# Stage 2 loads keys and values piece by piece, the last stage's first tiles lie beside it in SBUF, and out-projection begins with the first 1024 tokens

## Chip, cores and metric

One core of a Trainium2 chip runs the whole block. The metric is the device time of one execution in microseconds (us); of several runs the median stands.

## What is computed

One layer over 2048 tokens of width 1024, in float32. The reference, cut:

```python
h = _rmsnorm(x, ln1_g[l])
p = h @ w_in[l]
y_rwkv = _rwkv7_time_mix(p[..., :RWKV_COLS], ...)      # 8 heads x 64, recurrent over tokens
y_sb = _stick_breaking_attention(p[..., RWKV_COLS:], sb_gain[l])
x = x + jnp.concatenate([y_rwkv, y_sb], axis=-1) @ w_out[l]
h = _rmsnorm(x, ln2_g[l])
x = x + jnp.square(jax.nn.relu(h @ w_up[l])) @ w_down[l]
...
# in _stick_breaking_attention, for each block of queries:
z = jnp.einsum('bhqd,bhkd->bhqk', q[:, :, start:end], k[:, :, :end]) * scale
log_beta = jax.nn.log_sigmoid(z)
log_keep = jnp.where(causal, log_beta - z, 0.0)
log_a = log_beta + lax.cumsum(log_keep, axis=3, reverse=True) - log_keep
att = jnp.where(causal, jnp.exp(log_a), 0.0)
outs.append(jnp.einsum('bhqk,bhkd->bhqd', att, v[:, :, :end]))
```

Attention is causal: the output of the first tokens needs only the first keys and values.

## The kernel before, in words

Three stages follow each other; DRAM tensors carry data between them.

**Stage 1** projects the input and runs the recurrence, in four blocks of 512 tokens with two halves each. Its last part is `chain` of block 3, half 1: four chunks (names 310 to 313), each a row of small dependent steps: matmuls `Xp` (L557), `R` on VectorE (L570), `Up` (L572), a copy to `UV` on ScalarE (L573), `Sp` (L577), the state `S` on VectorE (L579). No later chunk can begin before `S` of the one before. Results go to the DRAM tensors `yd`, `vrd`, `bond`.

**Stage 2** is the attention: 4 query blocks b of 512, 4 pairs of heads hp, and for each the key blocks j = b down to 0, which makes 40 steps (b,hp,j). A step has four **fronts** (128 queries each): matmuls `z` (L271, L273), two sigmoids `keep` and `ga` on ScalarE (L275, L277), a scan `E` on VectorE (L281), a product into `ga` on GpSimd (L282). One step later come its **backs**: transposes `tr` (L297), a copy `th` on VectorE or ScalarE (L301, L302), matmuls into `OT` (L304). At the end of a (b,hp) `finish` copies OT (`ots`, L308), transposes it (`o`, L310), copies it (`osb`, L312) and stores it in the DRAM tensor `sbd` (L313). All 16 key tiles and 16 value tiles of the whole sequence stay in SBUF, and `load` fetches each once.

**Stage 3** begins with the out-projection. For each of 16 token tiles of 128, `mixed` loads `y` (from `yd` and `sbd`), `v`, `g` and `b` and normalizes y: means and squares (L86 to L93), a power on GpSimd (L96), products (L97 to L103). `prep` transposes y (`ytr`, L115) and splits it into `yh` and `yl` (L116, L117). `outproj` makes 2 x 24 matmuls `op` per tile (L30 to L32) against the weights `wo` (high half) and `wol` (low half). The weights come as eight pieces `wor` of 512 KB through two slots, called `xin`; each piece is converted on ScalarE (L199, L205) and subtracted on VectorE or GpSimd (L200, L206). The tiles of one half (1024 tokens) come first and go to the DRAM tensor `x2d`; those of the other stay in SBUF (`acc`) and go on to the MLP (`up`, `down`), which then takes the first half from `x2d`. Before, the half that came first was tokens 1024 to 2047.

The order on each engine is made by a scheduler from the data dependences, the memory that tiles share, and its own timing model; engines and the SP queue then run in that order. Pools have a left and a right side of SBUF. A tile whose memory overlaps that of an earlier pool waits for the tiles there.

Of the kernel before, what the change touches and what calls it, by code (L numbers as in the profile page):

```python
# [8 lines left out]
F32 = mybir.dt.float32  # L9
# [47 lines left out]
        nc.scalar.copy(hi,ps)  # L57
        nc.vector.tensor_tensor(out=lo,in0=ps,in1=hi.bitcast(F32),op=ALU.subtract)

def stage3(tc,consts,x,ys,w_out,g2,w_up,w_down,gf,gnw,gnb,gaincol,out,x2d,VB=1):  # L60

    yd,vrd,bond,gd,sbd=ys
    nc=tc.nc; V=nc.vector; P=nc.gpsimd; A=nc.scalar; TE=nc.tensor
    with ExitStack() as ctx:
        rctx=ExitStack()
        rp=rctx.enter_context(tc.tile_pool(name="s3r",bufs=1,reuse_waits="tile",side="right"))
        wol=rp.tile([128,8,1024],F32R,name="wol")
        gnwb=rp.tile([128,512],F32,name="gnw"); gnbb=rp.tile([128,512],F32,name="gnb")
        nc.sync.dma_start(out=gnwb,in_=gnw.to_broadcast([128,512]))
# [33 lines left out]
            V.tensor_tensor(out=yr,in0=yr,in1=gt_,op=ALU.mult)  # L103
            return yt
        def prep(half,tt,sp,rp):
            gt=half*8+tt
            yt=mixed(gt,sp,rp)
            xt=rp.tile([128,1024],F32,tag="xin",name=f"x3_{gt}",bufs=2)
            nc.sync.dma_start(out=xt,in_=x[128*gt:128*gt+128])
            yh=sp.tile([128,8,128],F32R,tag="yh",name=f"yh{gt}",bufs=2)  # L110
            yl=sp.tile([128,8,128],F32R,tag="yl",name=f"yl{gt}",bufs=2)
            for g in range(2):
                ps=pp.tile([128,4,128],F32,tag="tr",name=f"ytr{gt}{g}",bufs=2)
                for j in range(4):
                    TE.transpose(ps[:,j],yt[:,128*(4*g+j):128*(4*g+j+1)],consts['ident'])  # L115
                A.copy(yh[:,4*g:4*g+4],ps)  # L116
                V.tensor_tensor(out=yl[:,4*g:4*g+4],in0=ps,in1=yh[:,4*g:4*g+4].bitcast(F32),op=ALU.subtract)  # L117
            return yh,yl,xt
        def outproj(half,tiles,wo):

            for n in range(2):
                for tt,(yh,yl,xt) in tiles:
                    gt=half*8+tt; dst=xt if half else accs[0][tt]
                    ps=pp.tile([128,512],F32,tag="dn",name=f"op{gt}{n}",bufs=3)
                    for kt in range(8):
                        mm3(nc,ps,yh[:,kt],yl[:,kt],wo[0][n][kt],wo[1][:,kt,512*n:512*n+512],kt==0,kt==7)
                    V.tensor_tensor(out=dst[:,512*n:512*n+512],in0=ps,in1=xt[:,512*n:512*n+512],op=ALU.add)
                    if half and n: nc.sync.dma_start(out=x2d[128*tt:128*tt+128],in_=dst)
# [33 lines left out]
        def final(half,tt,sp):  # L162

            a=accs[half][tt]
            o=sp.tile([128,1024],F32,tag="xn" if tt%2 or not half else "wdf",name=f"fo{half}{tt}",bufs=2)
            ssq=sp.tile([128,2],F32,tag="ssqf",name=f"fssq{half}{tt}",bufs=4)
            for n in range(2):
                sl=slice(512*n,512*n+512)
                A.activation(o[:,sl],a[:,sl],AF.Square,accum_out=ssq[:,n:n+1])  # L169
            rs=sp.tile([128,1],F32,tag="rsf",name=f"frs{half}{tt}",bufs=4)  # L170
            P.tensor_tensor(out=rs,in0=ssq[:,0:1],in1=ssq[:,1:2],op=ALU.add)  # L171
            P.tensor_scalar(rs,rs,1.0/D,1e-5,ALU.mult,ALU.add)  # L172
            P.tensor_tensor(out=rs,in0=rs,in1=consts['mhalf'],op=ALU.pow)  # L173
            r0=1024*half+128*tt
            for n in range(2):
                sl=slice(512*n,512*n+512)
                if n and tt<7:
                    A.activation(o[:,sl],a[:,sl],AF.Copy,scale=rs)
                    P.tensor_tensor(out=o[:,sl],in0=o[:,sl],in1=gfb[:,sl],op=ALU.mult)  # L179
                else: V.scalar_tensor_tensor(out=o[:,sl],in0=a[:,sl],scalar=rs,in1=gfb[:,sl],op0=ALU.mult,op1=ALU.mult)  # L180
                nc.sync.dma_start(out=out[r0:r0+128,sl],in_=o[:,sl])
# [62 lines left out]
def stage2(tc,consts,kd,qd,vd,sbd,cfg=None):  # L244

    nc=tc.nc; V_=nc.vector; A=nc.scalar; P=nc.gpsimd; TE=nc.tensor
    g=dict(GA=9,E=6,TH=4,QB=3,DV=(1,4,7))
    g.update(cfg or {})
    with ExitStack() as ctx:
        sp=ctx.enter_context(tc.tile_pool(name="s2",bufs=1,reuse_waits="tile"))  # L250
# [5 lines left out]
        for k in keeps: P.memset(k[:,:,512:513],1.0)  # L256

        pad=pp.tile([128,1],F32,name="pad"); V_.memset(pad,0.0)
        kv={}; cnt=[0,0]
        def load(hp,j):  # L260
            K=sp.tile([128,512],F32,name=f"K{hp}{j}"); V=sp.tile([128,4,128],F32,name=f"V{hp}{j}")
            nc.sync.dma_start(out=K,in_=kd[hp][:,512*j:512*j+512])
            nc.sync.dma_start(out=V,in_=vd[hp][:,4*j:4*j+4])
            kv[hp,j]=(K,V)
        def front(b,hp,j,Q,carry,i):

            n=f"{b}{hp}{j}"; K=kv[hp,j][0]
            W=128*(i+1) if j==b else 512; o=512-W
            z=pz.tile([128,2,512],F32,tag="z",name=f"z{n}{i}",bufs=2)
            for h in range(2):  # L270
                TE.matmul(z[:,h,0:W],lhsT=Q[64*h:64*h+64,128*i:128*i+128],rhs=K[64*h:64*h+64,0:W],start=True,stop=j<b,skip_group_check=True)  # L271
            if j==b:
                for h in range(2): TE.matmul(z[:,h,W-128:W],lhsT=consts['identr'],rhs=consts['cmask'],start=False,stop=True,skip_group_check=True)  # L273
            s=keeps[cnt[0]%2]; cnt[0]+=1
            A.activation(s[:,:,o:512],z[:,:,0:W],AF.Sigmoid,scale=-0.125)  # L275
            ga=sp.tile([128,2,512],F32,tag="ga",name=f"ga{n}{i}",bufs=g['GA'])
            A.activation(ga[:,:,o:512],z[:,:,0:W],AF.Sigmoid,scale=0.125)  # L277
            E=sp.tile([128,2,513],F32,tag="E",name=f"E{n}{i}",bufs=g['E'])
            for h in range(2):
                init=1.0 if j==b else carry[i][h]  # L280
                V_.tensor_tensor_scan(E[:,h,o:513][:,::-1],s[:,h,o:513][:,::-1],pad.to_broadcast([128,W+1]),init,ALU.mult,ALU.bypass)  # L281
            P.tensor_tensor(out=ga[:,:,o:512],in0=ga[:,:,o:512],in1=E[:,:,o+1:513],op=ALU.mult)  # L282
            carry[i]=[E[:,h,o:o+1] for h in range(2)]
            return ga,o
        def back(b,hp,j,gas,OT,kt):

            n=f"{b}{hp}{j}"; V=kv[hp,j][1]
            i0=kt if j==b else 0; q0=128*i0
            for u in range(2):

                c0=max(i0,2*u)
                if c0>=2*u+2: continue
                tr=pt.tile([128,2,256],F32,tag="tr",name=f"tr{n}{kt}{u}",bufs=2)
                for h in range(2):
                    for i in range(c0,2*u+2):
                        ga,o=gas[i]
                        TE.transpose(tr[:,h,128*(i-2*u):128*(i-2*u)+128],ga[:,h,o+128*kt:o+128*kt+128],consts['ident'])  # L297
                th=sp.tile([128,2,256],F32,tag="th",name=f"th{n}{kt}{u}",bufs=g['TH'])
                q=slice(128*(c0-2*u),256); qq=slice(128*c0,256*u+256)
                cnt[1]+=1  # L300
                if cnt[1]%8 in g['DV']: V_.tensor_copy(out=th[:,:,q],in_=tr[:,:,q])  # L301
                else: A.copy(th[:,:,q],tr[:,:,q])  # L302
                for h in range(2):
                    TE.matmul(OT[64*h:64*h+64,qq],lhsT=V[:,kt,64*h:64*h+64],rhs=th[:,h,q],start=j==b and kt==0 and u==0,stop=j==0 and kt==3 and u==1,skip_group_check=True)  # L304
        def finish(b,hp,OT):
# [4 lines left out]
            for i in range(4): TE.transpose(o[:,i],ots[:,128*i:128*i+128],consts['ident'])  # L310
            osb=sp.tile([128,4,128],F32,tag="osb",name="osb"+n,bufs=2)
            A.copy(osb,o)  # L312
            nc.sync.dma_start(out=sbd[512*b:512*b+512,128*hp:128*hp+128].rearrange("(i p) d -> p i d",i=4),in_=osb)  # L313

        late=[None]
        def step(new):
            prev,late[0]=late[0],new
            for i in range(4):
                if new:
                    b,hp,j,Q,carry,gas,st=new  # L320
                    gas.append(front(b,hp,j,Q,carry,i))
                if prev:
                    b,hp,j,Q,carry,gas,st=prev
                    if j==b and i==0: st.append(pp.tile([128,512],F32,tag="OT",name=f"OT{b}{hp}",bufs=1))
                    back(b,hp,j,gas,st[0],i)
                    if j==0 and i==3: finish(b,hp,st[0])
        for b in range(4):
            for hp in range(4):
                load(hp,b)
                Q=sp.tile([128,512],F32,tag="Q",name=f"Q{b}{hp}",bufs=g['QB'])  # L330
                nc.sync.dma_start(out=Q,in_=qd[hp][:,512*b:512*b+512])
                carry=[None]*4; st=[]
                for j in range(b,-1,-1): step((b,hp,j,Q,carry,[],st))
        step(None)

def sb_consts(tc,cp,c):
# [332 lines left out]
def hybrid_block(tc, x, smalls, w_in, wd, wa, wg, g1, g2, gnw, gnb, w_out, w_up, w_down, gf, out):  # L669
    nc = tc.nc  # L670
    with ExitStack() as ctx:
# [13 lines left out]
        with tc.tile_pool(name="c1", bufs=1, reuse_waits="tile") as c1:  # L685
            rw_consts(tc, c1, c, smalls, wd, wa)
            stage1(tc, c, x, w_in, kd, qd, vd, scr, yd, vrd, bond, gd, wg, g1)
        stage2(tc, c, kd, qd, vd, sbd)
        stage3(tc, c, x, (yd, vrd, bond, gd, sbd), w_out, g2, w_up, w_down, gf, gnw, gnb, c["gain"], out, x2d)


def columns(a):
# [37 lines left out]
```

## Time and profile before

| | |
|---|---|
| median of 3 runs | 3343.86 us (3341.51 to 3344.73) |
| the profiled execution's own time | 3338.49 us |
| its span, first to last instruction | 3336.7 us |
| TensorE (PE) busy | 3166.1 us, 95% of the span |
| VectorE (DVE), GpSimd (POOL), ScalarE (ACT) busy | 2010.7, 1245.4, 1167.7 us |
| mean granted TensorE clock | 0.969 of full |

Stage 1 ends with the chain at about 1115 us, stage 2 runs from there to about 1665, out-projection to about 1920, the MLP to the end. The profile's shares are means over all of these; the two joints between the stages are read in their own stretches.

### The profile page before, as it was taken

To read this page: it belongs to the slowest core of one execution; us is meant where nothing else is said; L and a number is where in the kernel's file an instruction comes from. 1 tells how busy PE (TensorE), PEld (TensorE's weight loads), DVE (VectorE), ACT (ScalarE), POOL (GpSimd) and SP (SyncE) were. 2 spreads that over 40 slices of the span, in tenths; PEclk is the share of its full clock that TensorE was granted. 3 is DMA by queue.
4 is the path that set the end of the run, shared out by engine and by line. 5 is a ranking of instruction groups with operands and counts; after the bars stand their busy time and mean duration, and the time that the engine had idled before them with its cause. 6 is when DMAs were issued, how large, how long until landed. Compare 5 with 4: busy or idle time off the path is not lost. (4 is left out here: it accounts for less than half of the span.)

```text
span 3336.7 us, 45433 instructions
## 1 busy us (share of the span) xinstructions
PE 3166.1 (95%) x17504; PEld 2398.0 (72%) x17504; DVE 2010.7 (60%) x3139; ACT 1167.7 (35%) x2192; POOL 1245.4 (37%) x1089
## 2 busy tenths in 40 slices
PE   8999999999998799999959999999999999999998
PEld 6677767777777544444448788888888888888887
DVE  4674575476375477778566555555555755555555
ACT  4434443443442476667522221111111411111112
POOL 5444444443442354555455432222222422222223
PEclk9999999999998799999979999999999999999999
DMA  3342242232232400000065221111111421111111
GB/s 100 101 120 74 85 131 75 83 121 83 73 100 66 136 23 17 14 10 7 4 199 165 89 76 51 51 45 45 45 51 48 158 79 51 51 45 45 44 44 63
DMA packets 146729, 239.30 MB, mean 72 GB/s; under 512 B 50000, under 2 KB 58192, under 8 KB 146512
## 3 DMA queue, kind: packets, MB, share of 16 engines
q1 hardware_dynamic: 146512, 236.39, 22.7%
q8 instruction: 138, 2.26, 0.3%
q14 instruction: 79, 0.65, 0.1%
HBM read 190.14 MB, written 46.20 MB: 71 GB/s over the span
## 5 line engine op out<-in xcount | busy, mean ns | idle before, releaser
L160 DVE TENSOR_TENSOR acc<-acc,dn 128x512 f32<-128x512 f32 x512 | 344.5, 685 | 411.2 <-PE dn L32 405.6
L282 POOL TENSOR_TENSOR ga<-ga,E 128x1024 f32<-128x1024 f32 (+3 forms) x160 | 274.5, 1726 | 275.6 <-ACT ga L277 124.5
L145 ACT ACTIVATE r<-up 128x512 f32<-128x512 f32 x128 | 75.6, 592 | 615.4 <-PE up L32 615.4
L148 DVE TENSOR_TENSOR m<-r 128x512 f32<-128x512 f32 x128 | 190.9, 1492 | 113.5 <-ACT r L145 113.5
L281 DVE TENSOR_TENSOR_SCAN E<-keep,E,pad 128x513 f32<-128x513 f32 x192 | 232.4, 1263 | 36.4 <-ACT keep L275 36.4
L304 PE MATMUL OT<-th,V 128*64 128x256 f32 (+1 forms) x1152 | 179.5, 392 | 18.2 <-DVE th L301 17.8
L297 PEld LDWEIGHTS tr<-ident,ga 128*128 128x128 f32 x1088 | 114.5, 140 | 105.6 <-issue 94.1
L297 PE MATMUL tr<-ident,ga 128*128 128x128 f32 x1088 | 181.5, 287 | 5.4 <-DVE th L301 2.2
L271 PE MATMUL z<-K,Q 64*128 64x512 f32 (+3 forms) x640 | 159.8, 582 | 11.4 <-DMA Q<-qd 7.7
L275 ACT ACTIVATE keep<-z 128x1024 f32<-128x1024 f32 (+3 forms) x160 | 144.7, 906 | 72.1 <-PE z L273 31.0
L149 DVE TENSOR_TENSOR gl<-m,gh 128x512 fp32r<-128x512 f32 x128 | 148.4, 1160 | 11.6 <-ACT gh L146 0.9
L277 ACT ACTIVATE ga<-z 128x1024 f32<-128x1024 f32 (+3 forms) x160 | 143.7, 904 | 29.1 <-PE tr L297 28.4
L304 PEld LDWEIGHTS OT<-th,V 128*64 128x64 f32 x1152 | 57.6, 134 | 103.4 <-issue 40.1
L302 ACT COPY th<-tr 128x512 f32<-128x512 f32 (+1 forms) x180 | 101.2, 566 | 75.8 <-PE tr L297 74.7
L386 POOL TENSOR_TENSOR wls<-wfs,whs 128x512 fp32r<-128x512 f32 x64 | 84.3, 1318 | 109.1 <-ACT whs L385 100.8
L281 DVE TENSOR_TENSOR_SCAN E<-keep,pad 128x129 f32<-128x129 f32 (+3 forms) x128 | 97.6, 806 | 42.0 <-ACT keep L275 31.1
L535 DVE TENSOR_TENSOR tm<-Am,Xs 128x240 f32<-128x240 f32 (+27 forms) x248 | 106.1, 428 | 23.4 <-DMA Am<-scrA 17.1
L536 DVE TENSOR_TENSOR Xs<-Xs,tm 128x240 f32<-128x240 f32 (+27 forms) x248 | 113.5, 458 | 6.3
L30 PE MATMUL ips<-hT,whs 128*128 128x512 f32 x256 | 108.4, 423 | 0.5 <-ACT whs L385 0.4
L32 PE MATMUL ips<-hT,wls 128*128 128x512 f32 x256 | 107.9, 421 | 0.6 <-POOL wls L386 0.6
L301 DVE COPY th<-tr 128x512 f32<-128x512 f32 (+1 forms) x108 | 69.8, 647 | 63.1 <-PE tr L297 57.9
L30 PE MATMUL op<-wo,yh 128*128 128x512 f32 x256 | 103.4, 404 | 3.3 <-ACT yh L116 3.3
(1265 smaller groups left out, 8675.6 us busy)
## 6 DMA issues: line engine op xcount, KB each, us to landing
wfs<-w_in SPq DMA_DIRECT2D x64, 256.0 KB, 2.9
x<-x SPq DMA_DIRECT2D x32, 256.0 KB, 3.0
wfr<-w_in SPq DMA_DIRECT2D x32, 256.0 KB, 2.7
wfk<-w_in SPq DMA_DIRECT2D x32, 256.0 KB, 2.7
wfv<-w_in SPq DMA_DIRECT2D x32, 256.0 KB, 2.7
wfsv<-w_in SPq DMA_DIRECT2D x32, 256.0 KB, 2.8
x<-x SPq DMA_DIRECT2D x16, 512.0 KB, 3.6
out<-fo SPq DMA_DIRECT2D x32, 256.0 KB, 2.4
```

The lines of the kernel that those rows point to most:

```text
L30: nc.tensor.matmul(ps,lhsT=lh,rhs=rh,start=first,stop=False)
L148: V.tensor_tensor(out=m,in0=r,in1=r,op=ALU.mult)
L149: V.tensor_tensor(out=gl[:,bl],in0=m,in1=gh[:,bl].bitcast(F32),op=ALU.subtract)
L160: V.tensor_tensor(out=a,in0=a,in1=ps,op=ALU.add)
L271: TE.matmul(z[:,h,0:W],lhsT=Q[64*h:64*h+64,128*i:128*i+128],rhs=K[64*h:64*h+64,0:W],start=True,stop=j<b,skip_group_check=True)
L275: A.activation(s[:,:,o:512],z[:,:,0:W],AF.Sigmoid,scale=-0.125)
L277: A.activation(ga[:,:,o:512],z[:,:,0:W],AF.Sigmoid,scale=0.125)
L281: V_.tensor_tensor_scan(E[:,h,o:513][:,::-1],s[:,h,o:513][:,::-1],pad.to_broadcast([128,W+1]),init,ALU.mult,ALU.bypass)
L282: P.tensor_tensor(out=ga[:,:,o:512],in0=ga[:,:,o:512],in1=E[:,:,o+1:513],op=ALU.mult)
L297: TE.transpose(tr[:,h,128*(i-2*u):128*(i-2*u)+128],ga[:,h,o+128*kt:o+128*kt+128],consts['ident'])
L304: TE.matmul(OT[64*h:64*h+64,qq],lhsT=V[:,kt,64*h:64*h+64],rhs=th[:,h,q],start=j==b and kt==0 and u==0,stop=j==0 and kt==3 and u==1,skip_gr ...
L536: V.tensor_tensor(out=X[:,0:m,i+1:],in0=X[:,0:m,i+1:],in1=tm[:,0:m,i+1:],op=ALU.add)
```

## The change

`stage2` keeps four slots of keys and four of values and loads a piece for each step, 40 of each in place of 16; the queries have two slots in place of three; the store of `osb` is issued by ScalarE and not by SP. The right-side pool of stage 3 (`s3r`: the low weights `wol`, the inputs of `mixed`, `xin`, and now `yh` and `yl`) is opened before stage 2. The half that out-projection takes first is now tokens 0 to 1023. The amount of arithmetic is the same.

```diff
-def stage3(tc,consts,x,ys,w_out,g2,w_up,w_down,gf,gnw,gnb,gaincol,out,x2d,VB=1):
+def stage3(tc,consts,x,ys,w_out,g2,w_up,w_down,gf,gnw,gnb,gaincol,out,x2d,rp,rctx,VB=1):
...
-        rctx=ExitStack()
-        rp=rctx.enter_context(tc.tile_pool(name="s3r",bufs=1,reuse_waits="tile",side="right"))
...
-            gt=half*8+tt
+            gt=8-half*8+tt
...
-            yh=sp.tile([128,8,128],F32R,tag="yh",name=f"yh{gt}",bufs=2)
-            yl=sp.tile([128,8,128],F32R,tag="yl",name=f"yl{gt}",bufs=2)
+            yh=rp.tile([128,8,128],F32R,tag="yh",name=f"yh{gt}",bufs=2)
+            yl=rp.tile([128,8,128],F32R,tag="yl",name=f"yl{gt}",bufs=2)
...
-            r0=1024*half+128*tt
+            r0=1024*(1-half)+128*tt
...
-    g=dict(GA=9,E=6,TH=4,QB=3,DV=(1,4,7))
+    g=dict(GA=9,E=6,TH=4,QB=2,DV=(1,4,7),KV=4)
...
-        def load(hp,j):
-            K=sp.tile([128,512],F32,name=f"K{hp}{j}"); V=sp.tile([128,4,128],F32,name=f"V{hp}{j}")
+        def load(b,hp,j):
+            n=f"{b}{hp}{j}"
+            K=sp.tile([128,512],F32,tag="K",name="K"+n,bufs=g['KV']); V=sp.tile([128,4,128],F32,tag="V",name="V"+n,bufs=g['KV'])
             nc.sync.dma_start(out=K,in_=kd[hp][:,512*j:512*j+512])
             nc.sync.dma_start(out=V,in_=vd[hp][:,4*j:4*j+4])
-            kv[hp,j]=(K,V)
+            return K,V
...
-            nc.sync.dma_start(out=sbd[512*b:512*b+512,128*hp:128*hp+128].rearrange("(i p) d -> p i d",i=4),in_=osb)
+            A.dma_start(out=sbd[512*b:512*b+512,128*hp:128*hp+128].rearrange("(i p) d -> p i d",i=4),in_=osb)
...
-                load(hp,b)
...
-                for j in range(b,-1,-1): step((b,hp,j,Q,carry,[],st))
+                for j in range(b,-1,-1): step((b,hp,j,Q,*load(b,hp,j),carry,[],st))
...
+        rctx = ExitStack()
+        rp = rctx.enter_context(tc.tile_pool(name="s3r", bufs=1, reuse_waits="tile", side="right"))
         stage2(tc, c, kd, qd, vd, sbd)
```

Lines of the changed kernel stand up to two numbers lower than those named above in the rows of order that follow.

On PE, in chunk 310 of the last chain (z0000 is z of b=0, hp=0, j=0, front 0), the order before was:

```order
L557 MATMUL Xp310_10571<-S_165,AR313_9519 128x128
L572 MATMUL Up310_10580<-R310_10579,XT31_9692 32x64 x8
L569 MATMUL Xp310_10571<-UV310_9270,P13100_9362 32x64 x2
L569 MATMUL Xp310_10571<-UV310_9270,P13110_9449 32x64 x2
L569 MATMUL Xp310_10571<-UV310_9270,P13120_9536 32x64 x2
L569 MATMUL Xp310_10571<-UV310_9270,P13130_9580 32x64 x2
```

And now:

```order
L555 MATMUL Xp310_10571<-S_165,AR313_9519 128x128
L270 MATMUL z0000_10862<-K000_10858,Q00_10856 128x128 x2
L272 MATMUL z0000_10862<-cmask_97,identr_95 128x128 x2
L270 MATMUL z0001_10874<-K000_10858,Q00_10856 128x256 x2
L272 MATMUL z0001_10874<-cmask_97,identr_95 128x128 x2
L570 MATMUL Up310_10580<-R310_10579,XT31_9692 32x64 x8
L270 MATMUL z0002_10886<-K000_10858,Q00_10856 128x384 x2
```

The z of 11 fronts (0000 to 0003, 0100 to 0103, 0200 to 0202) now stand among the matmuls of chunks 310 and 311; before, the first stood behind the last chunk. Their ScalarE, VectorE and GpSimd rows moved with them: in these two chunks 20 sigmoids stand between ScalarE's copies of the chain.

On VectorE, right behind the last state `S` of the chain, now (gm0 and gm1 are means of the out-projection's tiles 0 and 1, th00011 a copy of a back of stage 2):

```order
L577 TENSOR_TENSOR S_165<-SD313_10775,Sp313_10808 64x4x64 x2
L300 COPY th00000_10934<-tr00000_10929 128x512
L280 SCALAR_TENSOR_TENSOR E0203_11119<-keep1_10851,pad_10854 128x513 x2
L198 TENSOR_TENSOR wol_15484<-wor00_15515,wo00_15517 128x2x512
L84 TENSOR_REDUCE gm0_15565<-y3_0_15556 128x8
L300 COPY th00011_10971<-tr00011_10966 128x512
L85 TENSOR_SCALAR gm0_15565<-gm0_15565 128x8
L86 TENSOR_TENSOR y3_0_15556<-y3_0_15556,gm0_15565 128x512
L84 TENSOR_REDUCE gm1_15618<-y3_1_15609 128x8
L280 SCALAR_TENSOR_TENSOR E0300_11154<-keep0_10850,pad_10854 128x129 x2
```

Four rows further on stands `ots00`, the finish of the first (b,hp). Before, the rows of wol, gm and y stood behind the last `ots33` of stage 2. All of `mixed` for tiles 0 and 1, up to the last product (L103), now stands inside stage 2; SP has the loads for it, and pieces wor00 to wor02, between the loads of keys and values.

On SP, in the middle of stage 2, the loads now run V202, Q21, K212, V201, K211, V200 (the steps run 202, 201, 200, 212, 211): a key piece is issued beside the value piece of two steps before. There were no such loads here before.

On PE, at the end of stage 2, now (op00 is tile 0, column half 0):

```order
L309 MATMUL o33_15472<-ident_60,ots33_15470 128x128 x4
L113 MATMUL ytr00_15595<-ident_60,y3_0_15556 128x128 x4
L113 MATMUL ytr01_15602<-ident_60,y3_0_15556 128x128 x4
L30 MATMUL op00_15715<-wo00_15517,yh0_15593 128x512
L31 MATMUL op00_15715<-wol_15484,yh0_15593 128x512
L113 MATMUL ytr10_15648<-ident_60,y3_1_15609 128x128 x4
```

Before, the transposes of tile 8 stood here, whose y was loaded behind the last store of stage 2. Pieces wor03 and wor10 to wor13 are still loaded behind the last key and value loads, each when a slot is free.

## Rows read from the trace of the kernel before

**Rows 1.** The page's head and its part 1 (busy us, share, instructions).
```profile
span 3336.7 us, 45433 instructions
...
PE 3166.1 (95%) x17504; PEld 2398.0 (72%) x17504; DVE 2010.7 (60%) x3139; ACT 1167.7 (35%) x2192; POOL 1245.4 (37%) x1089
```

**Rows 2.** Windows: length, busy us of PE, PEld, DVE, ACT, POOL, clock, DMA.
```profile
1050.00:1115.00 65.00, 49.45 (x511) 42.83 (x509) 11.85 (x25) 11.48 (x20) 5.01 (x10) 0.65 0.12 33
...
1150.00:1175.00 25.00, 24.16 (x150) 12.45 (x150) 19.62 (x27) 18.22 (x28) 13.74 (x10) 1.00 0.11 33
1175.00:1200.00 25.00, 22.89 (x143) 11.12 (x141) 19.56 (x24) 17.13 (x27) 13.55 (x9) 1.00 0.11 33
...
1665.00:1708.00 43.00, 3.36 (x17) 2.40 (x14) 23.87 (x26) 13.16 (x21) 20.49 (x13) 0.57 0.65 207
```

**Rows 3.** Timeline, joint of stages 1 and 2: start, us, engine, line, idle before.
```profile
1064.18 1.16 PE L557 MATMUL Xp<-S,AR 128*128 128x128 f32 x8
...
1113.35 1.91 PE L582 MATMUL Xp<-UV,P 128*64 128x64 f32 x16
1122.92 0.80 PE L271 MATMUL z<-K,Q 64*128 64x128 f32 x4 [7.66 <-DMA Q<-qd]
...
1148.91 0.66 PE L310 MATMUL o<-ident,ots 128*128 128x128 f32 x4 [0.80 <-DVE ots L308]
```

**Rows 4.** Timeline, joint of stages 2 and 3, PE and the fourth `op` sum.
```profile
1663.93 1.40 PE L304 MATMUL OT<-th,V 128*64 128x256 f32 x8
...
1703.04 1.97 PE L115 MATMUL ytr<-ident,y 128*128 128x128 f32 x8 [36.26 <-DVE y L103]
1707.59 0.80 PE L30 MATMUL op<-wo,yh 128*128 128x512 f32 x1 [2.58 <-ACT yh L116]
...
1740.60 0.68 DVE L127 TENSOR_TENSOR x<-op,x 128x512 f32<-128x512 f32 x1
```

**Rows 5.** Timeline, the same joint, other engines.
```profile
1667.84 0.50 SPq L69 DMA_DIRECT2D gnw<-gnw  x1
...
1680.71 0.68 DVE L86 TENSOR_REDUCE gm<-y 128x8 f32<-128x512 f32 x1
...
1692.16 2.35 POOL L26 TENSOR_TENSOR wu00l<-wu00f,wu00h 128x1024 fp32r<-128x1024 f32 x1
1692.22 3.37 DVE L97 TENSOR_TENSOR y<-y,gs 128x1024 f32<-128x1024 f32 x1 [1.18 <-POOL gs L96]
```

**Rows 6.** Tile wor: ns min/median/max, first and last start us; landing times.
```profile
L200 DVE TENSOR_TENSOR wol<-wor,wo x2: 1224/1224/1225, 1679.6 to 1703.9; 128x1024 fp32r<-128x1024 f32 x2
L200 POOL TENSOR_TENSOR wol<-wor,wo x2: 2339/2352/2365, 1681.0 to 1707.1; 128x1024 fp32r<-128x1024 f32 x2
...
DMA to landing us min/median/max: 3.8/5.4/10.0
```

**Rows 7.** Tile op, the first of its three kinds of matmul.
```profile
L30 PE MATMUL op<-wo,yh x256: 389/395/796, 1707.6 to 1917.7; 128*128 128x512 f32 x128
```

**Rows 8.** Groups by line and form, 1120 to 1665 us: busy us, mean ns, idle before.
```profile
L275 ACT ACTIVATE keep<-z 128x1024 f32<-128x1024 f32 x112 | 115.7, 1035 | 39.2 <-PE z L271 21.7 <-PE z L273 7.9 <-issue 2.5
...
L275 ACT ACTIVATE keep<-z 128x256 f32<-128x256 f32 x16 | 6.4, 399 | 7.6 <-PE z L273 7.4
```

**Rows 9.** Lines 93, 97 and 103: ns min/median/max, first and last start us.
```profile
L93 DVE TENSOR_REDUCE gs<-gsq x64: 403/411/421, 1684.9 to 1889.1; 128x4 f32<-128x256 f32 x64
L97 DVE TENSOR_TENSOR y<-y,gs x16: 1217/1226/3369, 1692.2 to 1896.7; 128x1024 f32<-128x1024 f32 x16
L103 DVE TENSOR_TENSOR y<-y,g x16: 675/682/692, 1702.3 to 1900.2; 128x512 f32<-128x512 f32 x16
```

**Rows 10.** Part 5 of the page, the products of stage 2 on GpSimd.
```profile
L282 POOL TENSOR_TENSOR ga<-ga,E 128x1024 f32<-128x1024 f32 (+3 forms) x160 | 274.5, 1726 | 275.6 <-ACT ga L277 124.5
```

**Rows 11.** DMA issues from 1150 to 1660 us: KB each, us to landing; and line 313's issue.
```profile
Q<-qd SPq DMA_DIRECT2D x10, 256.0 KB, 2.6
...
L313 SPq DMA_DIRECT2D sbd<-osb x16: 359/360/370, 1150.2 to 1667.4; - x16
```

More of the change, by code (lines that the diff above doesn't have):

```diff
@@ L122, in outproj @@
                 for tt,(yh,yl,xt) in tiles:
-                    gt=half*8+tt; dst=xt if half else accs[0][tt]
+                    gt=8-half*8+tt; dst=xt if half else accs[0][tt]
                     ps=pp.tile([128,512],F32,tag="dn",name=f"op{gt}{n}",bufs=3)
@@ L258, in stage2, with front @@
         pad=pp.tile([128,1],F32,name="pad"); V_.memset(pad,0.0)
-        kv={}; cnt=[0,0]
-        def load(hp,j):
-            K=sp.tile([128,512],F32,name=f"K{hp}{j}"); V=sp.tile([128,4,128],F32,name=f"V{hp}{j}")
+        cnt=[0,0]
+        def load(b,hp,j):
+            n=f"{b}{hp}{j}"
+            K=sp.tile([128,512],F32,tag="K",name="K"+n,bufs=g['KV']); V=sp.tile([128,4,128],F32,tag="V",name="V"+n,bufs=g['KV'])
             nc.sync.dma_start(out=K,in_=kd[hp][:,512*j:512*j+512])
             nc.sync.dma_start(out=V,in_=vd[hp][:,4*j:4*j+4])
-            kv[hp,j]=(K,V)
-        def front(b,hp,j,Q,carry,i):
-            n=f"{b}{hp}{j}"; K=kv[hp,j][0]
+            return K,V
+        def front(b,hp,j,Q,K,carry,i):
+            n=f"{b}{hp}{j}"
             W=128*(i+1) if j==b else 512; o=512-W
@@ L284, in front, with back @@
             return ga,o
-        def back(b,hp,j,gas,OT,kt):
-            n=f"{b}{hp}{j}"; V=kv[hp,j][1]
+        def back(b,hp,j,V,gas,OT,kt):
+            n=f"{b}{hp}{j}"
             i0=kt if j==b else 0; q0=128*i0
@@ L319, in step @@
                 if new:
-                    b,hp,j,Q,carry,gas,st=new
-                    gas.append(front(b,hp,j,Q,carry,i))
+                    b,hp,j,Q,K,V,carry,gas,st=new
+                    gas.append(front(b,hp,j,Q,K,carry,i))
                 if prev:
-                    b,hp,j,Q,carry,gas,st=prev
+                    b,hp,j,Q,K,V,carry,gas,st=prev
                     if j==b and i==0: st.append(pp.tile([128,512],F32,tag="OT",name=f"OT{b}{hp}",bufs=1))
-                    back(b,hp,j,gas,st[0],i)
+                    back(b,hp,j,V,gas,st[0],i)
                     if j==0 and i==3: finish(b,hp,st[0])
@@ L687, in hybrid_block @@
             stage1(tc, c, x, w_in, kd, qd, vd, scr, yd, vrd, bond, gd, wg, g1)
+        rctx = ExitStack()
+        rp = rctx.enter_context(tc.tile_pool(name="s3r", bufs=1, reuse_waits="tile", side="right"))
         stage2(tc, c, kd, qd, vd, sbd)
-        stage3(tc, c, x, (yd, vrd, bond, gd, sbd), w_out, g2, w_up, w_down, gf, gnw, gnb, c["gain"], out, x2d)
+        stage3(tc, c, x, (yd, vrd, bond, gd, sbd), w_out, g2, w_up, w_down, gf, gnw, gnb, c["gain"], out, x2d, rp, rctx)
 def columns(a):
```

## Prediction

> **What bounds the kernel now.** I read the page first: PE is busy 95% of 3336.7 us [rows 1], so time can only come from stretches where PE stands still, and those have to be found by place. The windows show two. At the joint of stages 1 and 2 PE is busy 49 of 65 us at a mean clock of 0.65, while DVE and ACT are busy 12 and 11 us [rows 2]: every engine waits for another one's small step. The timeline shows this chain ending at 1115.26 us (1113.35 + 1.91) and the first z at 1122.92, after 7.66 us of waiting for the load of Q [rows 3]. At the joint of stages 2 and 3 PE is busy 3.4 of 43 us while the DMA moves 207 GB/s [rows 2]. The last OT ends at 1665.33, the next transposes begin at 1703.04 after an idle 36.26 us that VectorE's last product of `mixed` ended, and the first op stands at 1707.59 [rows 4]. Everything that this product needs (loads, squares, power) begins only behind stage 2's last store [rows 5]. Between the joints PE is busy 47.05 of 50 us at full clock (the two windows from 1150 [rows 2]), so there is little to win there and something to lose.
>
> **The joint of stages 2 and 3.** Take T as the end of the last OT. Before, the fourth op sum (tiles 0 and 1 of the order, both column halves) is taken out of PSUM from 1740.60, which is T + 75.3 [rows 4]. Now y of two tiles is ready at T, and half of the weights' pieces are loaded. What is late next is the rest of the weights. Five pieces are left, through two slots, and one slot takes wor03, wor11 and wor13 one after the other, each when the one before is converted. T to the end of wor01's conversion: `ots`, `o`, two `ytr`, two `yh`, the cast and GpSimd's subtraction of 2.35 us [rows 6], which I put at 7 us. Then three rounds of landing (median 5.4 us [rows 6]) and conversion (a cast of about 1 us, a subtraction of 1.22 or 2.35 [rows 6], and a place in the queue: 4.4 together): 3 x 9.8 = 29.4. Behind the last piece come 6 matmuls of tile 0 and 24 of tile 1; out-projection's 768 matmuls take 210.1 us (1707.6 to 1917.7 [rows 7], transposes included), 0.27 each, so 8 us. Sum: T + 44.4, against T + 75.3: a gain of 30.9. Out-projection started at a low clock before, and the stop-and-go start now will give some of that again: I take 28. Bounds: with landings of 3.8 us the sum is T + 40 (gain 36), with 10.0 T + 58 (gain 17) [rows 6]. Later tiles cost what they did; PE sets their pace, and the swap of halves only changes which rows are loaded.
>
> **The joint of stages 1 and 2.** Eleven fronts now run inside chunks 310 and 311, from 1064 us on [rows 3]. They fill idle time, but stand in the chain's queues. On ACT 20 sigmoids stand between the chain's copies; of 128x256 to 128x1024, they take 0.40 to 1.04 us [rows 8], 0.72 in the mean, 14.3 together. If each held up the chain by its whole length, it would end 14.3 later; if all fell into gaps, not at all. Going through the two chunks row by row, about half are in the way, because DVE's scans and PE's z stand in the same places: 8 us. So the chain ends at about 1123.
>
> What follows is no longer free either. Behind the chain DVE has wol and gm0 ahead of th00011, and gm0 waits for a load issued behind the chain's last store. The same series of loads before took from 1667.84 to the reduction at 1680.71, 12.9 us [rows 5]; then gm1, whose load is issued later, then short rows up to ots00. I put `o00` at 21 us behind the chain's end; the bounds are 14 (the loads alone) and 30. Before, it was 33.65 us behind it (1148.91 - 1115.26 [rows 3]), with two fronts fewer done, worth 2.5 us on PE. Gain: 33.65 + 2.5 - 8 - 21 = 7 us, from -8 (14.3 and 30) to +22 (0 and 14).
>
> **The cost inside stage 2.** PE has no new row there, the others have. DVE: per tile one reduction (0.68 [rows 5]), three products (0.68 each [rows 9]), L97 (1.23) and four L93 (0.41 each), 5.6 us, twice, and wol of wor00 (1.22 [rows 6]): 12.4 us, nearly all in the first 75 us or so of stage 2. DVE is idle for 10.8 of the 50 us from 1150 [rows 2], some 16 in 75, but not where it suits.
>
> Nine of these rows read two SBUF operands beside a busy GpSimd, and the trace shows what that can do: L97 takes 1.23 us in the median but 3.37 at 1692.22, where a GpSimd row of 2.35 us had started at 1692.16 [rows 5, 9]. It looks as if DVE waited for the end of that row. The Trainium skill has the rule for this (SBUF — State Buffer, section SBUF: two separate sides): VectorE with two SBUF inputs and GpSimd share one pair of ports under an exclusive lock, and the loser waits for the whole instruction. The trace agrees, 3.37 being about 2.3 + 1.2. By that rule the insertions cost more than their sum. From the rows: GpSimd's products last 1.73 us in the mean [rows 10] and GpSimd is busy 27.3 of 50 us [rows 2], so the mean wait is 0.55 x 0.86 = 0.47, 4 us for nine, at worst 9 x 1.73 = 15.6.
>
> So DVE gets 17 us more work (12.4 to 28) against some 16 idle. I charge PE 6 of it; below 0, above all 28. The first reads of `sbd` stand in ACT's queue soon after the store: 3 us (0 to 8). The 16 stores that ACT issues cost at most 16 x 0.36 = 5.8, by the price on SP [rows 11]; ACT has idle time there, I take 1. Together 10 us, of bounds 0 to 42.
>
> The 40 loads of keys and 40 of values I cost at nothing. A step lasts (1665.33 - 1122.92) / 40 = 13.6 us [rows 3, 4] and a load of this size lands in 2.6 [rows 11]; a piece waits for the slot of the one four steps before, which is free two steps (27 us) ahead of its use at the least. If that cover went, each of the 36 steps behind the first four would show 2.6 us. Two slots for Q are enough by the same argument. The MLP's order is unchanged: nothing.
>
> **Sum.** 28 + 7 - 10 = 25 us gained. The profiled execution took 3338.49, its span 3336.7; the median of the runs is 3343.86, 5.4 above it. I take the difference from the median: 3343.86 - 25 = **3319 us**.
>
> **Rivals.** (a) *The weights' slots keep the second gap.* If landings stay at the 10.0 us of a full queue, the joint gives 17, less 2 for the clock: 15 + 7 - 10 = 12, 3332 us. For it: up-projection weights and the next tiles' y are loaded at the same moment. Against: the burst of before also had the first two tiles and three more pieces in it.
>
> (b) *The lock gives the gain back.* If DVE's whole 28 us reach PE, the cost is 32 with the other items, the sum 28 + 7 - 32 = 3, and nothing can be told from no change: 3341 us. For it: L97's 3.37. Against: GpSimd is idle for almost half of that stretch.
>
> (c) *Slower: the ring of four slots.* SP runs in order, and rows of `mixed` that wait for their own slot (the second and third v) stand ahead of keys and values. If that makes the pieces late, each of 36 steps pays up to 2.6 us: 94 us against a gain of 35 and a cost of 10, 3413 us. It decides the sign from 25 / 36 = 0.7 us per step. Against it: the order has over a step to spare each time, and only two such rows are there.
>
> (d) *The chain isn't held up and the loads are early:* 33 + 22 - 3 = 52, 3292 us. For it: ACT and DVE are busy under a fifth of the window from 1050 [rows 2].
>
> **Chances and range.** My forecast with its own bounds (3303 to 3330) 0.60; (a) 0.15; (b) 0.09; (c) 0.07; (d) 0.09. The range 3301 to 3336 takes in the forecast and (a), leaves out (c) and most of (b) and (d). A change of 0.2%, 6.7 us, is about what a measurement of this kernel can tell from none. Faster by more: forecast, (a) and (d), 0.84; within it: most of (b), 0.08; slower: (c), and a (b) with a late chain, 0.08.
>
> **What would show it.** Right: z rows between `Xp` and `Up` from about 1064 us; the chain's end near 1123; `o00` some 20 us behind it, with VectorE's gm0 waiting for a load; the first op within 5 us of the last OT, with waits of PE for wol until T + 37; the fourth op sum near T + 45. Wrong: a chain that ends later than 1130; PE waiting for K or V in stage 2; PE busy under 44 of 50 us in the first 75 us of stage 2; op waiting beyond T + 50.

## The result and the profile after

The changed kernel takes 3305.34 us in the median (3304.51 to 3307.57, 4 runs), the kernel before 3343.56 us beside it: a ratio of 0.989, 95% interval 0.987 to 0.990, 38 us less. A second series (e12 below) gave 0.988 (0.986 to 0.990). The forecast was 3319 us, with a range of 3301 to 3336.

The profiled executions differ by less, 3336.7 - 3304.0 = 32.7 us of span; this is the sum that places can explain. The other 5.5 us are the choice of execution: their own times, 3338.49 and 3306.05 us, lay 5.1 below and 0.7 above the medians (less 0.3 us between these times and the spans).

Page of the changed kernel, head and part 1:

```profile
span 3304.0 us, 45579 instructions
PE 3164.0 (96%) x17504; PEld 2395.6 (73%) x17504; DVE 2018.1 (61%) x3139; ACT 1168.4 (35%) x2192; POOL 1243.6 (38%) x1089
```

PE does the same work ([rows 1]: 3166.1); only its idle time shrank. The windows say where (columns as in [rows 2]; the last window is the 43 us behind the last OT):

```profile
1050.00:1115.00 65.00, 54.24 (x521) 42.25 (x520) 26.07 (x46) 24.37 (x40) 15.95 (x17) 0.76 0.33 90
...
1663.00:1706.00 43.00, 31.76 (x127) 23.28 (x128) 31.05 (x46) 18.17 (x32) 26.26 (x16) 0.92 0.68 226
```

In the window from 1050 DVE and ACT are twice as busy as before, and PE's clock is 0.76 and not 0.65. At the joint of stages 2 and 3 PE is busy 31.8 of 43 us; before, 3.4 [rows 2].

Timeline of the changed kernel from the end of the chain to the first `o`; to be set beside [rows 3]:

```profile
1065.65 0.49 PE L270 MATMUL z<-K,Q 64*128 64x128 f32 x4
...
1120.47 1.91 PE L580 MATMUL Xp<-UV,P 128*64 128x64 f32 x16
...
1131.71 1.04 ACT L197 CAST wo<-wor 128x1024 fp32r<-128x1024 f32 x1 [4.57 <-DMA wor<-w_out]
1132.78 1.23 DVE L198 TENSOR_TENSOR wol<-wor,wo 128x1024 fp32r<-128x1024 f32 x1 [3.28 <-DMA v<-vrd]
1133.08 0.70 PE L303 MATMUL OT<-th,V 128*64 128x128 f32 x4 [4.88 <-ACT th L301]
...
1143.09 1.07 PE L309 MATMUL o<-ident,ots 128*128 128x128 f32 x4
```

The chain ends at 1122.38. The 7.66 us of waiting for Q are gone, and a stall of 4.88 us has come: ScalarE stands at the cast of the first weight piece until that piece lands (at 1131.68), and the copy `th` that PE needs stands behind it. VectorE's `wol` starts 0.03 us behind the end of this cast, on which it depends; the load of v that its row names landed only at 1134.38, so the wait is the cast's.

The next joint, beside [rows 4]:

```profile
1661.33 1.40 PE L303 MATMUL OT<-th,V 128*64 128x256 f32 x8
...
1665.88 0.50 PE L30 MATMUL op<-wo,yh 128*128 128x512 f32 x1 [0.83 <-ACT yh L114]
...
1678.06 3.26 DVE L204 SCALAR_TENSOR_TENSOR wol<-wor,gain,wo 128x512 fp32r<-128x512 f32 x2
...
1680.71 0.51 PE L31 MATMUL op<-wol,yh 128*128 128x512 f32 x1 [1.90 <-DVE wol L204]
...
1691.51 1.88 PE L113 MATMUL ytr<-ident,y 128*128 128x128 f32 x8 [3.20 <-DVE y L101]
...
1705.72 0.69 DVE L125 TENSOR_TENSOR x<-op,x 128x512 f32<-128x512 f32 x1
```

With T = 1662.73, the end of the last OT, the first op stands at T + 3.2 and the fourth op sum (last line) at T + 43.0; before, at T + 42.3 and T + 75.3. Of the 11.2 us that PE stands idle in this window, 6.5 are waits for weights, 3.2 the wait for y of the third tile (the row from 1691.51), the rest waits for `ots` and `yh`.

Stage 2 can be read step by step: one `o` closes each of the 16 (b,hp), and the intervals between them repeat from one execution to the next to about 0.1 us where the granted clock is full. (In e12, the same kernel again, one of them takes 26.8 us and not 25.9, at a mean clock of 0.94.) Before they are, from o03 on, 26.0, 23.7, 25.7, 28.3 us; now 28.0, 25.9, 25.7, 28.3, and the others differ by 0.3 at the most (the first apart: 13.3 and 12.1). Only where the rows of the first two tiles stand, between o03 and o11, has stage 2 become slower.

### The profile page after: what moved, and what is told of

It is laid out like the page before. It is cut to its first block, busy times and chain, and to the rows that moved or that the text cites. A ratio compares the mean times of both kernels' runs of the same rounds, so it can differ in the third digit from the quotient of the medians.

```text
span 3304.0 us, 45579 instructions
## 1 busy us (share of the span) xinstructions
PE 3164.0 (96%) x17504; PEld 2395.6 (73%) x17504; DVE 2018.1 (61%) x3139; ACT 1168.4 (35%) x2192; POOL 1243.6 (38%) x1089
## 5 line engine op out<-in xcount | busy, mean ns | idle before, releaser
L276 ACT ACTIVATE ga<-z 128x1024 f32<-128x1024 f32 (+3 forms) x160 | 143.2, 901 | 28.3 <-PE tr L296 27.9
```

## The experiments

The kernel before varied more in these sessions than in the first runs (3333 to 3361 us over all), so edits worth less than 10 us are decided by place, each in one profiled execution. This table is worked out from the timelines of all profiled executions (us; "chain": from the first Xp of chunk 310 to the chain's end; T: end of the last OT; "sum": the fourth op sum; "op end": start of the last op):

| | chain | to o00 | o00 to o01 | o01 to o33 | T to sum | T to op end |
|---|---|---|---|---|---|---|
| before | 51.1 | 33.7 | 13.3 | 503.9 | 75.3 | 252.8 |
| the change | 57.8 | 20.7 | 12.1 | 508.3 | 43.0 | 222.1 |
| e12, again | 57.8 | 20.0 | 11.7 | 509.3 | 42.5 | 220.8 |
| e1 last half first | 57.8 | 20.7 | 12.1 | 510.5 | 42.8 | 218.9 |
| e6 z on the right | 52.1 | 36.2 | 13.3 | 508.7 | 43.3 | 219.0 |
| e9 two Q slots alone | 73.9 | 11.5 | 11.5 | 508.4 | 73.3 | 248.4 |
| e7 rows behind (0,0) | 57.0 | 11.8 | 17.6 | 508.3 | 43.3 | 220.1 |
| e10 rows behind (3,2) | 60.8 | 11.2 | 11.5 | 510.9 | 42.4 | 222.3 |
| e14 rows behind (3,3) | 57.8 | 11.8 | 11.5 | 508.9 | 61.8 | 236.4 |
| e8 three xin slots | 57.8 | 20.4 | 12.2 | 508.1 | 33.8 | 214.1 |
| e11 = e10 + e8 | 60.7 | 11.2 | 11.5 | 510.9 | 33.7 | 216.9 |
| e13 = e7 + e8 | 56.9 | 11.7 | 20.7 | 508.4 | 34.3 | 215.0 |
| e5 two K/V slots | 69.1 | 20.5 | 11.8 | 512.5 | 37.7 | 215.3 |
| e4 store by SP | 57.8 | 20.3 | 12.2 | 508.1 | 43.3 | 222.5 |

**e1: tokens 1024 to 2047 first again.**

```diff
-            gt=8-half*8+tt
+            gt=half*8+tt
-            r0=1024*(1-half)+128*tt
+            r0=1024*half+128*tt
```

> The changed kernel, but out-projection again begins with tokens 1024 to 2047. Theory (the tiles' own data are what the early start needs): y of the first tiles waits for stage 2's last store again, so the first op stands near T + 41 (T the end of the last OT), and the fourth op sum, 96 matmuls of 0.27 us later, near T + 65 in place of T + 43; about 21 us of the gain are lost: 3324 to 3332 us. Rival (the two weight pieces loaded beside stage 2 are what counts): fourth op sum below T + 50 and 3305 to 3311 us.

Measured: 3304.61 us, ratio 0.989 (0.987 to 0.991); T + 42.8. The theory fell. Tiles 8 and 9 are tokens 1024 to 1279, which belong to query block 2, and that is done a whole block (45 + 57 + 53 + 55 us) ahead of T. Their rows then slow down the interval from o23 to o30, 61.8 us in place of 55.1: PE waits more, and its rows take 56.3 us in place of 52.0 at a granted clock of 0.92 and not 1.00. Between o03 and o11 the intervals are those of before again (26.0, 23.7). The order of the halves is worth nothing here; that y and weights are prepared beside stage 2, whichever tiles they are, is what counts at this joint.

**e6: the PSUM pool of z on the other side, no front in the chain.**

```diff
-        pz=ctx.enter_context(tc.tile_pool(name="p2z",...,space=PS))
+        pz=ctx.enter_context(tc.tile_pool(name="p2z",...,space=PS,side="right"))
-        pt=ctx.enter_context(tc.tile_pool(name="p2t",...,space=PS,side="right"))
+        pt=ctx.enter_context(tc.tile_pool(name="p2t",...,space=PS))
```

> The changed kernel, but the PSUM pool of z takes the other side, so that no front stands in the last chain. Theory (the two joints' gains add): the chain ends at 1115 again and o00 stands near 1149 to 1153, the joint of stages 2 and 3 keeps its gain of 31 us: 3313 to 3319 us. Rival (the fronts in the chain bring nothing, since they hold the chain up by as much): 3303 to 3308 us.

Measured: 3319.1 us, 0.993 (0.991 to 0.995). The later joint keeps its gain (T + 43.3), and the chain takes 52.1 us again. The time agrees, but not all of it for the reason given: chunk 310 also starts later (at 1072.06; in the other executions of the table at 1060.8 to 1065.6), and PE's order in stage 1 ahead of it differs too. The places separate the two: from the start of chunk 310 to o01 this kernel takes 101.6 us and the change 90.6, so the fronts in the chain are worth 11.0 us at this joint.

**e9: the kernel before with two slots for Q, nothing else.**

```diff
-    g=dict(GA=9,E=6,TH=4,QB=3,DV=(1,4,7))
+    g=dict(GA=9,E=6,TH=4,QB=2,DV=(1,4,7))
```

> The kernel before with one number changed: two slots for Q in place of three. Its order of instructions then has the 11 fronts in the last chain. Theory (the fronts' overlap is a gain by itself, and the rows of the first tiles behind the chain only take from it): chain's end 7 us later, o00 near chain + 15, 8 to 16 us faster than before: 3328 to 3336 us, joint of stages 2 and 3 unchanged. Rival (the gain of that joint comes from the loads piece by piece): 3341 to 3346 us.

Measured: 3336.83 us, 0.998 (0.996 to 1.000), far less than expected. This edit alone moves the 11 fronts into the chain, but PE then waits in the middle of it. PE of this kernel, behind chunk 310:

```profile
1091.78 0.80 PE L271 MATMUL z<-K,Q 64*128 64x128 f32 x4 [8.39 <-DMA Q<-qd]
...
1092.99 2.02 PE L557 MATMUL Xp<-S,AR 128*128 128x128 f32 x8
```

The third Q is issued at 1086.08, behind 26 loads of keys and values that fill their 16 tiles (251 GB/s from 1064 to 1100; the changed kernel moves 84), and the chain's next Xp stands behind the z that needs it. Behind this wait the granted clock was lower as well: chunk 311 takes 18.4 us at 0.50, in the change 14.8 at 0.77. The chain takes 73.9 us, and o00 comes at 1149.23, where it was before. So neither of my two theories: the two Q slots move the fronts, and the loads piece by piece make that pay. The second half of that is read from the two traces; a kernel with these two edits alone wasn't run.

**e7: the rows of the first weight piece and of tiles 0 and 1 queued behind the finish of (0,0).** `held(b,hp)` puts ScalarE's and VectorE's rows behind the copies of that finish.

```diff
+                    with held(0,0) if n==0 and k==0 else ExitStack():
                         A.copy(hi,src)
                         (P if k else V).tensor_tensor(out=lo,...)
-            ready=[prep(*todo[0],wp,rp)]
+            with held(0,0): ready=[prep(*todo[0],wp,rp)]
```

> The changed kernel, but the ScalarE and VectorE rows of the first weight piece and of tiles 0 and 1 are queued behind the first finish of stage 2. Theory: PE's stall of 4.88 us behind the chain goes, because ScalarE no longer stands at a cast that waits for its load: o00 near 1138 to 1140 and 3299 to 3302 us. Rival (the stall covers a wait of the same length for the copies th, or comes back as lost cover later in stage 2): within 2 us of 3305.

Measured: 3305.01 us, 0.989 (0.987 to 0.991), not to be told from the change; by place it is clear. o00 stands 11.8 us behind the chain's end in place of 20.7, at 1131.78. More than half of these 8.9 us is given back at once: o00 to o01 takes 17.6 us in place of 12.1. There PE waits 3.24 us for a `th` behind these rows, and the granted clock is 0.81 and not 0.90. So the stall covered work that costs 5.5 us elsewhere, and its removal brings T 4.4 us nearer to the start of chunk 310.

**e8: three xin slots.** The rows of norm2 move into the same slots to make room.

```diff
-                src=rp.tile([128,2,512],F32,tag="xin",...,bufs=2)
+                src=rp.tile([128,2,512],F32,tag="xin",...,bufs=3)
```

> The changed kernel with three xin slots in place of two (the normalized rows of norm2 share them, since SBUF has no room for both). Theory (rounds of the weights' slots set the start of out-projection): four pieces left behind T through three slots, the longest row two rounds: 7 + 2 x 9.8 + 8 = T + 34.6 for the fourth op sum in place of T + 43, 8 us less. Rival (the pieces share the DMA, more at once land later; or y of the next tiles and VectorE are late next): T + 40 to T + 43, 0 to 3 us less.

Measured: 3295.26 us, 0.9856 (0.9837 to 0.9875), with the fourth sum at T + 33.8 and PE without one wait above 1.2 us from T to it. Window of this kernel, 43 us behind its T (1659.67):

```profile
1660.00:1703.00 43.00, 37.62 (x165) 28.68 (x166) 32.60 (x46) 17.94 (x31) 25.83 (x16) 0.96 0.75 263
```

PE is busy 37.6 us and not 31.8; from T to the end of out-projection it takes 214.1 us, 8.0 less. A third slot takes away what the rounds forecast, and the DMA had room for it (263 GB/s against 226). That the number of slots alone decides is not shown: e5 below comes to T + 37.7 with two.

**e12: the changed kernel again, in the session of e8, e10 and e11.**

> The changed kernel once more, beside the runs that follow, as their mark. Both theories: a ratio of 0.989 to the kernel before, and the same places to within 1 us (chain's end at 57.8 us behind the start of chunk 310, o00 20.7 behind the end, T + 43.0 for the fourth op sum).

Measured: 3303.34 us, 0.988 (0.986 to 0.990); the places agree to 1.3 us.

**e10 and e11: the first piece's rows behind (0,3), those of tiles 0 and 1 behind (3,2), the last 45 us of stage 2; e11 with three slots too.**

```diff
+                    with held(0,3) if n==0 and k==0 else ExitStack():
...
+            with held(3,2): ready=[prep(*todo[0],wp,rp)]
```

> The changed kernel; ScalarE's and VectorE's rows of the first weight piece are queued behind the finish of (0,3), those of tiles 0 and 1 behind the finish of (3,2), that is in the last 45 us of stage 2, where VectorE is busy 26.7 us. Theory (their cost is their place: behind the chain and in block 1 VectorE is on the path, in the tail it isn't): o00 near 12 us behind the chain's end in place of 20.7, no PE waits for th between (0,3) and (1,1), the last OT 10 to 14 us earlier, T + 43 as before: 3291 to 3296 us. Rival (in the tail each row delays the last th, and the second tile's v and g wait for their one slot): the last OT 3 to 6 us earlier at most, or the first op over 10 us behind T: 3299 to 3305 us.

> The two edits before together (rows held back, three xin slots). Theory (their gains lie at different places and add): the last OT as with the held rows, the fourth op sum as with three slots: 3282 to 3290 us. Rival (one hides the other): the better of the two alone.

Measured: 3301.82 us, 0.9869 (0.9854 to 0.9885), and 3297.93 us, 0.9857 (0.9842 to 0.9872). o00 and the intervals behind o03 came out as expected (26.5, 23.7), but the tail pays. PE of e10, behind o32:

```profile
1616.30 1.12 PE L309 MATMUL OT<-th,V 128*64 128x256 f32 x4 [4.88 <-DVE th L306]
```

The last interval takes 50.8 us in place of 45.3. The chain takes 60.8 in place of 57.8: chunks 311 and 312 ran at a granted clock of 0.68 and 0.63, in the change at 0.77 and 0.80 (why it was lower is open). From the start of chunk 310 T comes 4.6 us earlier and not 10 to 14: the rival held, in e11 too, which is no better than e8.

**e14: the rows of tiles 0 and 1 behind the last finish.** As e10, with `held(3,3)`.

> The changed kernel (two xin slots); the rows of tiles 0 and 1 on ScalarE and VectorE are queued behind stage 2's last finish, those of the first weight piece behind (0,3), so that only loads and the first weight piece are done beside stage 2. Theory (weights' slots set the start of out-projection, so y computed beforehand is worth little): first op at T + 15 to T + 20, fourth op sum at T + 44 to T + 50, stage 2 without the 10 us of these rows: within 4 us of the changed kernel. Rival (y computed beforehand is the gain): first op at T + 20 or later and fourth op sum beyond T + 55, 3310 us or more.

Measured: 3311.19 us, 0.990 (0.988 to 0.993). The theory fell, the rival held. T is 9.0 us earlier than in the change, from the start of chunk 310, but the first transposes of y wait 22.5 us for VectorE, the first op stands at T + 29, the sum at T + 61.8. Behind T the rows of y take turns with the weights' conversions on VectorE and ScalarE, and the weights' rounds don't hide that. So of the 32.3 us at the fourth sum, loads and the first weight piece beside stage 2 give 75.3 - 61.8 = 13.5, and y computed there 18.8. Net it is far less, since the rows of y also delay T: from the start of chunk 310 the end of out-projection comes 5.3 us later here than in the change, 4.5 of which are the slow stretch described at the end, and the medians differ by 5.9.

**e13: e7 and e8 together.**

> Three xin slots, and the rows of the first weight piece and of tiles 0 and 1 queued behind the finish of (0,0). Theory (the rows' 5.5 us behind (0,0) and 4.5 us in block 1 stay, the PE stall behind the chain goes): last OT 592.3 us behind the start of chunk 310 in place of 596.8, fourth op sum at T + 34: 4 to 5 us less than with three slots alone, ratio 0.984 to 0.985. Rival (ends as the version with rows held to the tail did): 0.9855 to 0.9865.

Measured: 3297.67 us, 0.986 (0.984 to 0.989): no better than e8. o00 to o01 took 20.7 us, 3.1 more than in e7, with gm1 waiting 2.63 us for its y (1.41 in e7) in front of the copies. The granted clock of this interval was 0.67, in e7 0.81, and PE's rows took 16.3 us in place of 13.7. The rival's ratio came.

**e5 and e4: two slots of keys and of values; stores by SP.** One execution each.

```diff
-    g=dict(GA=9,E=6,TH=4,QB=2,DV=(1,4,7),KV=4)
+    g=dict(GA=9,E=6,TH=4,QB=2,DV=(1,4,7),KV=2)
```

```diff
-            A.dma_start(out=sbd[512*b:512*b+512,...],in_=osb)
+            nc.sync.dma_start(out=sbd[512*b:512*b+512,...],in_=osb)
```

> The changed kernel with two slots of keys and two of values in place of four. Theory (a key tile's slot is free one step of 13.6 us ahead, a value tile is used a step after its keys; a landing takes 2.6): the intervals between the 16 o rows of stage 2 stay within 0.5 us. Rival (the ring decides): each step shows up to 2.6 us, 38 steps, up to 99 us more.

> The changed kernel with the stores of osb issued by SP again. Theory (four slots of keys and values cover an SP queue that waits at a store): intervals between the o rows unchanged to 0.5 us, no difference in time. Rival (loads behind a waiting store come late): PE waits for K or Q, intervals up to 3 us longer at each of the 16 finishes.

Measured: 3309.86 and 3301.33 us. In both the intervals are those of the change to 0.3 us, but for one of e5's (47.4 in place of 42.9, below). Neither the ring nor the issuing engine costs stage 2 anything. What e5 lost lies elsewhere. ScalarE of e5 in chunk 310:

```profile
1067.50 1.04 ACT L24 CAST wu00h<-wu00f 128x1024 fp32r<-128x1024 f32 x1 [5.71 <-DMA wu00f<-w_up]
```

With the memory that the smaller ring freed, the first four weight pieces of the MLP (`wu00f` to `wu03f`) are loaded from 1061 us on and not behind T, and the first cast stands ahead of the first sigmoid and of the chain's copies: the chain takes 69.1 us, chunk 310 at a granted clock of 0.64 in place of 0.82.

The same loads are then missing behind T, and there e5 gains. Its 43 us behind T:

```profile
1674.00:1717.00 43.00, 37.31 (x165) 28.38 (x162) 30.09 (x50) 17.53 (x32) 21.95 (x17) 0.92 0.61 202
```

With two slots as in the change, PE is busy 37.3 us and not 31.8, the fourth sum stands at T + 37.7, and out-projection ends 6.8 us nearer to T. The five pieces land in 4.4 us in the median (5.3 in the change), GpSimd has fewer subtractions, and PE no longer waits for y. Which of these counts most was not separated, in a single execution; but at the end of out-projection 6.8 of the 8.0 us that a third slot brings come without it, once the MLP's pieces are out of the way.

## Why the prediction was right, and where not

The bound was read rightly: the gain came from the two joints, PE's work and the MLP stayed as they were. By terms, in the profiled executions:

| term | predicted | measured |
|---|---|---|
| joint of stages 2 and 3 | +28 (17 to 36) | +30.8 at the end of op (252.8 to 222.1), +32.3 at the fourth sum |
| joint of stages 1 and 2 | +7 (-8 to +22) | +7.4 at o01 (98.0 to 90.6 from the start of chunk 310, which is 0.4 later in this execution) |
| stage 2 | -10 (0 to -42) | -4.4 (o01 to o33) |
| sum | 25 | 33.8; less 0.4 for stage 1 and 0.7 behind out-projection, 32.7 of span |

**Weights' rounds: right in the sum, not the only limit.** T + 44.4 was worked out, T + 43.0 came, and PE waited for wol until T + 35.8 (37 was named). The three rounds of one slot took 11.6, 10.5 and 6.7 us in place of three times 9.8, so their agreement is in part luck. e8 shows that the slots count: one more takes 9.2 us away where the same sum gives 9.8. They are not all of it. e5 takes 5.3 us away with two slots, and e14 shows that without y the sum stands at T + 61.8; in the change itself PE waits 3.2 us for y of the third tile. The deduction of 3 us for the low clock was not needed; the clock did fall, to 0.83 from 1680 to 1700, but the whole gain of 30.8 is what stood there before the deduction.

**The chain held up by 8 us: right in size, wrong in the engine.** The stretch from chunk 310 to the chain's end takes 6.7 us longer; e6 shows 52.1 without fronts. The prediction priced ScalarE's sigmoids. Chunk 310 before and now (columns as in [rows 2]):

```profile
1064.18:1075.70 11.52, 7.84 (x93) 6.90 (x89) 2.22 (x4) 2.32 (x4) 1.22 (x2) 0.75 0.07 24
```

```profile
1064.57:1083.17 18.60, 18.31 (x146) 12.55 (x143) 11.95 (x18) 12.41 (x20) 8.52 (x8) 0.82 0.40 115
```

Now PE is busy almost throughout, with nine of the eleven z among the chain's matmuls, and ScalarE for 12.4 of 18.6 us: PE's own queue holds the chain up, by 7.1 us here. Chunk 311, with the other two z, takes 14.8 us in place of 15.1, since the granted clock was 0.77 there and before 0.51. The prediction had not counted this help of the clock.

**o00 21 us behind the chain: right in sum, wrong in the row.** VectorE did wait for a load, but at wol, ahead of gm0, and through ScalarE's cast. (gm0's own load landed at 1133.70, 0.9 us behind the start of wol, so gm0 alone would have waited about as long.) And I had not seen that ScalarE's cast of the same piece stands in front of `th`, which is what stopped PE for 4.88 us.

**Stage 2's cost: the mis-sized term.** It was the sum of 6 us for VectorE's rows, 3 for the first reads of `sbd` and 1 for the stores. The rows cost 4.2 us between o03 and o11. Part of the 6 was counted twice: five of the rows (wol, and for each tile gm and the first product, 4.0 of the 12.4 us) stand ahead of o00, and the 21 us held them already. e7, where they stand behind (0,0), pays 5.5 us there and 4.4 between o03 and o11. The reads of `sbd` cost nothing that can be seen: ScalarE waits 0.76 us for the first, and no wait of PE follows on it. That stores on ScalarE cost nothing, nor the loads of keys and values, is shown by the intervals and by e4 and e5. The sign named for a cost too high, PE busy under 44 of 50 us, was just missed: 66.4 of the first 75, which is 44.3 of 50. The loads of keys land in 2.9 us in the median, and so do those of values:

```profile
K<-kd SPq DMA_DIRECT2D x40, 256.0 KB, 2.9
```

**The lock** is there, but small in stage 2. VectorE and GpSimd of the changed kernel in block 1:

```profile
1221.03 1.99 POOL L281 TENSOR_TENSOR ga<-ga,E 128x1024 f32<-128x1024 f32 x1
1221.70 1.88 DVE L100 TENSOR_TENSOR y<-y,v 128x512 f32<-128x512 f32 x1
...
1224.95 0.65 PE L303 MATMUL OT<-th,V 128*64 128x256 f32 x4 [1.83 <-DVE th L300]
```

L100 takes 0.69 us elsewhere; here it ends 0.56 us behind the GpSimd row, and the `th` behind it makes PE wait. The Trainium skill's rule of the shared ports (SBUF — State Buffer, section SBUF: two separate sides) fits this row and the two L204 above, which took 3.26 us together where one takes 0.74, beside a GpSimd subtraction of 2.37. Of block 1's 4.2 us this row is 1.2.

**The swap of halves** was given nothing, rightly; but that the early start would have been possible without it, since block 2 is done long before T, the prediction didn't say. Nor did it see which number moves the fronts: the two slots for Q, which it passed over as harmless (e9).

**Rivals.** (a) fell: the pieces behind T landed in 5.3 us in the median, not 10. (b) and (c) fell by the intervals. (d) asked for a chain that isn't held up.

**The distance of 14 us** from forecast to result: 7.7 are the sum (32.7 - 25, of which 5.6 are stage 2 and 2.8 the deduction for the clock). The rest is the choice of executions: the profiled one of before was 5.4 us faster than the median from which the 25 us were taken off, and the gain between the medians is larger by about that than the gain between the profiles.

## What to carry to other kernels

Work brought beside an earlier stage pays where that stage's engines wait, and costs where its rows stand in an in-order queue in front of rows on the path: look for the first row that waits for a load, on every engine, not only the one that is short. A ring of buffers that fills behind a stage boundary limits the start by rounds (landing plus conversion). One slot more was worth 8 us here, more than holding rows back at any of the places tried; other loads kept out of the ring's way were worth 6.8 in e5, which lost more than that in the chain. When a row comes late though nothing in front of it changed, read the granted clock beside it as well as the waits (e9, e10, e13). And count a moved row once: either in the wait that it lengthens or in the stage where it stands.

## What the runs showed of the hardware that was not expected

In e5, e9 and e14 one stretch of stage 2 ran for 10.2 us at half of the full clock, the lower of its two levels, although nothing in it was changed; in all three it is the interval from o22 to o23, 47.4 us in place of 42.9. Windows of e9:

```profile
1410.00:1420.00 10.00, 8.35 (x54) 4.27 (x52) 10.00 (x10) 8.64 (x12) 6.60 (x4) 1.00 0.18 54
1420.00:1430.00 10.00, 8.64 (x38) 4.37 (x36) 4.76 (x8) 2.71 (x7) 3.99 (x3) 0.65 0.00 0
```

PE was busy 8.4 of the 10 us ahead of the fall. The eleven other profiled executions have 42.9 there. What decides it stays open; it is worth 4.5 us, as much as the smaller edits here. Without it e9's stage 2 from o01 to o33 takes 503.9 us, as before.
